# A two-layer hybrid decoder trunk: seven turned operands a layer through VectorE and DRAM, and another order of the column groups

## The chip, the cores and the metric

The kernel runs on one core of a Trainium2 chip. A core has a matrix engine (TensorE, PE in the profile; its weight loads are listed apart as PEld), three engines for element work (VectorE or DVE, ScalarE or ACT, GpSimd or POOL) and SyncE (SP), whose queue here issues nearly all transfers. Each engine works through its own instructions in order, and semaphores tie the engines together. On-chip data lie in SBUF (128 partitions); TensorE writes to PSUM.

The metric is the device time of one execution in microseconds; less is better.

## The reference

Two layers, 256 positions, width 1024, all in float32. In each layer one projection of the normalised input gives ten groups of 512 columns, three branches work on them, and a second projection adds the result to x:

```python
h = rms_norm(x, norm_g[l])
proj = h @ w_in[l]
q_a, k_a, v_a, q_h, f_h, i_h, q_m, z = jnp.split(proj, split_points, axis=-1)
# q_a, k_a: per-head RMS norm and partial rotary; 8 heads of 64
o_a = moba_attention(qa, ka, va).reshape(B, S, G)
o_h = hgrn2_chunkwise(q_h, f_h, i_h, lb_all[l])         # 4 heads of 128, gated recurrence
o_h = rms_norm(o_h, hgrn_o_norm[l])
kv_m = rms_norm(mem, mem_norm_g[l]) @ w_mem_kv[l]
o_m = memory_attention(rms_norm(q_m), rms_norm(k_m), v_m)  # 4 heads of 128, 256 memory tokens
y = jnp.concatenate([o_a, o_h, o_m], axis=-1) * jax.nn.silu(z)
x = x + y @ w_out[l]
```

With 256 positions and blocks of 256, MoBA has one block, so its attention is a plain causal one within it.

## The kernel before

**Weights.** All weight matrices stream through SBUF in 120 chunks of 128x1024 floats (512 KB). SyncE loads a chunk into `wr` (four buffers), ScalarE rounds it into `wh` (line 161, or 164 with a gain), VectorE makes the remainder `wl = wr - wh` (line 173, or 176 with a gain); `wh` and `wl` have three buffers each. A product is three matmuls: high x high, high x low, low x high. `slot` (line 206) runs twice a chunk: once a chunk it issues the next load, cast and remainder (`dma_to`, `h_to`, `l_to`: 5, 3 and 2 chunks ahead), and then `step` advances each of the active generators by one. So a `yield` in the code is about half a chunk of TensorE's time, and `yield 2` two halves.

**Groups.** `group_a` computes a column group with the result transposed (columns on partitions: F, Q, ZA, ZM), `group_b` with positions on partitions (KA, QA, IH, ZH, QM, VA). When a group's matmuls are out, a generator takes its accumulator: `g_f`, `g_q` and `g_hgrn` (the recurrent branch, "the scan"), `g_qk` (q and k of MoBA, then `g_moba` and its two `g_moba_unit`), `g_ih`, `g_va`, `g_zh` and `g_zt` (gates), `g_qm` (the memory's q, then two `g_mem_unit`), and at the start of a layer `g_km` and `g_vm` (the memory's k and v). Z stands for the gates, A, H and M for MoBA, HGRN and memory. The order of the groups in a layer is F Q ZA ZM KA QA IH ZH QM VA, then `w_out_phase` in the order H, A, M of the branches.

**Turned operands.** The norms need positions on partitions and the products need the head's columns there, so several tensors are transposed between. Five places do it on TensorE, 128x128 against `ident`, into a PSUM tile `sd` from which ScalarE and VectorE copy:

- `g_km`, line 611: kn, 8 transposes a layer, then `kmh` (line 612, with the gain) and `kml` (line 613);
- `g_qk`, line 919: k and q, 8 each, then `kT`, `qT` by ScalarE (line 920);
- `y_transpose`, line 731: zh (the gated output of HGRN), 8, then `yh`, `yl` (lines 734 and 735, with the gain of the out-norm);
- `g_qm`, line 1047: qm, 8, then `qmh`, `qml` (lines 1048 and 1049);
- `g_mem_unit`, line 1101: the softmax P of two heads, 8 transposes a unit, 16 a layer, then `PTh`, `PTl` (lines 1103 and 1104).

A sixth place, P of MoBA in `g_moba_unit`, goes another way: `across` (line 88). VectorE turns 32x32 blocks from the tensor into `blk` (one buffer, line 92), SyncE writes `blk` to a DRAM tile `there` (line 96) and reads it back by four transfers (line 99) that put the blocks on their partitions. The turned tensor then has its positions in an order of 32-wide pieces, and the matmul reads it through an access pattern of such pieces.

**What orders the work.** The instructions are traced in the order of the code; the build then orders each engine's queue by a simulated time line (`schedule_with_timeline_sim=True`), except those marked with `keep_in_program_order` (weight loads, matmuls of `mm_row`, the end of the last projection). Waits on names in `done` and on rooms (`room`, `take`) hold a generator back in the code: `P` has two tiles, `PTh` and `PTl` one each, `blk` one. The tag `qk` (one buffer) holds kn, kr of k, kr of q and qm in turn. The unit of MoBA waits before its exponentials until the gates ZM are done (line 964).

Of the kernel before, what the change touches and what calls it, by code (L numbers as in the profile page):

```python
# [45 lines left out]
def hymba_kernel(ctx: ExitStack, tc: tile.TileContext, x, mem, mem_t, positions, w_in, w_out, w_mem_kv,  # L46
# [34 lines left out]
    def rel(what="sd", n=1):  # L81
        held[what] -= n
# [5 lines left out]
    def across(dst, src, n):  # L88
        yield from room("blk")
        held["blk"] += 1  # L90
        blk = sb.tile([128, 4, n * 32], F32, name="blk", tag="blk", bufs=1)
        nc.vector.transpose(blk.rearrange("p c (n i) -> p c n i", n=n),
                            src.rearrange("p (n c i) -> p c n i", n=n, c=4))
        yield 2
        there = away.tile([4, 32, 4, n * 32], F32, name="there", tag="there", bufs=2)
        nc.sync.dma_start(there.rearrange("q j c r -> (q j) c r"), blk)
        yield 2
        for c in range(4):
            nc.sync.dma_start(dst[c * 32:c * 32 + 32], there[:, :, c].rearrange("q j r -> j q r"))
            if c % 2:  # L100
                yield
        rel("blk")

# [460 lines left out]
    def heads(t, n):  # L564
        return t.rearrange("p (h d) -> p h d", h=n)
# [13 lines left out]
    def g_km(l, acc):  # L579
# [23 lines left out]
        kmh = sb.tile([128, 4, 256], F32R, name="kmh", tag="kmh", bufs=1)  # L603
        kml = sb.tile([128, 4, 256], F32R, name="kml", tag="kml", bufs=1)
        g = gkq[:, l:l + 1]
        for t in range(2):
            ts = slice(t * 128, (t + 1) * 128)
            yield from room("sd")
            pt = side_tile()
            for h in range(4):  # L610
                nc.tensor.transpose(pt[:, h * 128:(h + 1) * 128], kn[:, t, h * 128:(h + 1) * 128], ident)
            nc.scalar.activation(kmh[:, :, ts], heads(pt, 4), AF.Copy, scale=g)
            nc.vector.scalar_tensor_tensor(kml[:, :, ts], in0=heads(pt, 4), scalar=g, in1=kmh[:, :, ts].bitcast(F32),
                                           op0=OP.mult, op1=OP.subtract)
            rel()
# [111 lines left out]
    def y_transpose(l, t, gain):  # L727
        yield from room("sd")
        pt = side_tile()
        for j in range(4):  # L730
            nc.tensor.transpose(pt[:, j * 128:(j + 1) * 128], zh[:, t, j * 128:(j + 1) * 128], ident)
        p3 = heads(pt, 4)
        oh, ol = (a[:, :, t * 128:(t + 1) * 128] for a in y_tiles(H_))
        nc.scalar.activation(oh, p3, AF.Copy, scale=gain)
        nc.vector.scalar_tensor_tensor(ol, in0=p3, scalar=gain, in1=oh.bitcast(F32), op0=OP.mult, op1=OP.subtract)
        rel()
        yield
        if t == 1:
            for k in range(4):
                done.add(f"y{4 * H_ + k}_{l}")  # L740


    def g_hgrn(l):
# [129 lines left out]
        yield 2  # L873
        for t in range(2):
            yield from y_transpose(l, t, gT[:, GR_O + l:GR_O + l + 1])


    def g_qk(l, q, acc):
# [35 lines left out]
        o = sb.tile([128, 4, 256], F32, name=tg, tag=(f"yl{M_}", f"yh{M_}")[q], bufs=1)  # L914
        for t in range(2):
            yield from room("sd")
            pt = side_tile()
            for p in range(4):
                nc.tensor.transpose(pt[:, p * 128:(p + 1) * 128], kr[:, t, p * 128:(p + 1) * 128], ident)  # L919
            nc.scalar.copy(o[:, :, t * 128:(t + 1) * 128], heads(pt, 4))  # L920
            rel()
            yield
# [28 lines left out]
    def g_moba_unit(l, u, P, mx):  # L951
# [12 lines left out]
        while f"z{M_}{l}" not in done:  # L964
            yield
# [36 lines left out]
    def g_moba(l):  # L1002
# [26 lines left out]
    def g_qm(l, acc):  # L1029
# [12 lines left out]
        for t in range(2):  # L1042
            ts = slice(t * 128, (t + 1) * 128)
            yield from room("sd")
            pt = side_tile()
            for h in range(4):
                nc.tensor.transpose(pt[:, h * 128:(h + 1) * 128], qm[:, t, h * 128:(h + 1) * 128], ident)
            nc.scalar.copy(qmh[:, :, ts], heads(pt, 4))
            nc.vector.tensor_tensor(qml[:, :, ts], heads(pt, 4), qmh[:, :, ts].bitcast(F32), op=OP.subtract)
            rel()  # L1050
# [6 lines left out]
    def g_mem_unit(l, u, qm, r, nr):  # L1057
# [35 lines left out]
        yield 2  # L1093
        yield from take("PTh", "PTl")
        PT = [sb.tile([128, 2, 2, 256], F32R, name=n, tag=n, bufs=1) for n in ("PTh", "PTl")]
        for b in range(2):
            yield from room("sd")
            pt = side_tile()
            for i in range(2):
                for t in range(2):  # L1100
                    nc.tensor.transpose(pt[:, i * 256 + t * 128:i * 256 + (t + 1) * 128],  # L1101
                                        P[:, t, i, b * 128:(b + 1) * 128], ident)
            nc.scalar.copy(PT[0][:, b], heads(pt, 2))
            nc.vector.tensor_tensor(PT[1][:, b], heads(pt, 2), PT[0][:, b].bitcast(F32), op=OP.subtract)
            rel()
# [86 lines left out]
    for l in range(DEPTH):  # L1192
# [4 lines left out]
        for gen in (A_, M_, lambda l, a: g_qk(l, 1, a), lambda l, a: g_qk(l, 0, a), g_ih, g_zh, g_qm, g_va):  # L1197
# [56 lines left out]
```

## Time and profile before

| | us |
|---|---|
| median of 3 runs | 403.14 |
| lowest and highest of them | 403.0, 404.85 |
| the profiled execution | 402.83 |
| its span in the trace | 401.0 |
| busy: TensorE, VectorE, ScalarE, GpSimd | 393.9, 310.4, 257.6, 56.4 |

The span is what the trace covers; 1.83 us of the execution lie around it. The granted clock is full (tenths of 9 or more in all slices of the page). A row of the groups reads: line, engine, operation, what it writes and reads, shapes, count, then busy time, mean ns of one, and idle time of the engine just before such instructions with what ended it. Busy time of TensorE counts overlapping instructions once; the mean of a matmul is its own length, which overlaps that of its neighbours, so what one costs is read from the distance of the starts or from the chain that ended last.

### The profile page before, as it was taken

To read this page: it belongs to the slowest core of one execution; us is meant where nothing else is said; L and a number is where in the kernel's file an instruction comes from. 1 tells how busy PE (TensorE), PEld (TensorE's weight loads), DVE (VectorE), ACT (ScalarE), POOL (GpSimd) and SP (SyncE) were. 2 spreads that over 40 slices of the span, in tenths; PEclk is the share of its full clock that TensorE was granted. 3 is DMA by queue.
4 is the path that set the end of the run, shared out by engine and by line. 5 is a ranking of instruction groups with operands and counts; after the bars stand their busy time and mean duration, and the time that the engine had idled before them with its cause. 6 is when DMAs were issued, how large, how long until landed. Compare 5 with 4: busy or idle time off the path is not lost.

```text
span 401.0 us, 7633 instructions
## 1 busy us (share of the span) xinstructions
PE 393.9 (98%) x2919; PEld 330.7 (82%) x2919; DVE 310.4 (77%) x602; ACT 257.6 (64%) x431; POOL 56.4 (14%) x79
## 2 busy tenths in 40 slices
PE   8999999999999999999999999999999999999996
PEld 5888888888887878888888888888888888787885
DVE  5789999978845989685676789898767658988653
ACT  6998757784556895553466676566654598748430
POOL 2014400605400011100000040000144001020000
PEclk9999999999999999999999999999999999999999
DMA  7976563544453397744454555634455427894402
GB/s 286 412 282 218 182 209 139 181 157 161 159 189 126 135 232 267 259 142 146 162 194 158 197 170 196 208 112 160 159 184 185 159 61 254 252 279 153 156 2 105
DMA packets 22629, 74.06 MB, mean 185 GB/s; under 512 B 2752, under 2 KB 5184, under 8 KB 22592
## 3 DMA queue, kind: packets, MB, share of 16 engines
q1 hardware_dynamic: 22304, 73.41, 54.3%
q8 instruction: 23, 0.38, 0.4%
q10 hardware_dynamic: 288, 0.15, 0.2%
q14 instruction: 14, 0.11, 0.1%
HBM read 69.36 MB, written 4.19 MB: 183 GB/s over the span
## 4 chain that ended last, share of the span: by engine, by line
PE 87%; DVE 8%; issue 1%; DMA 1%; POOL 1%; ACT 1%; DVEq 0%
PE acc L215 59%; PE acc L1138 16%; PE sd L215 5%; PE sd L219 3%; DVE wl L173 3%; DVE P L978 2%; DMA gT<-in_gains_dram 1%; PE sd L1101 1%; PE sd L428 1%; PE sd L919 1%; DVE zh L868 1%; POOL hgr L576 1%; DVE P L932 1%; ACT P L969 1%; DVE ssh L570 1%
## 5 line engine op out<-in xcount | busy, mean ns | idle before, releaser
L161 ACT CAST wh<-wr 128x1024 fp32r<-128x1024 f32 x104 | 109.2, 1052 | 85.2 <-PE acc L215 64.0
L173 DVE TENSOR_TENSOR wl<-wr,wh 128x1024 fp32r<-128x1024 f32 x104 | 126.9, 1221 | 39.5 <-ACT wh L161 39.0
L215 PE MATMUL acc<-wh,hT 128*128 128x512 f32 x384 | 123.0, 395 | 0.0
L215 PEld LDWEIGHTS acc<-wh,hT 128*128 128x128 f32 x384 | 71.8, 188 | 15.9 <-issue 1.3
L215 PE MATMUL acc<-wl,hT 128*128 128x512 f32 x192 | 75.8, 395 | 0.6 <-DVE wl L173 0.6
L215 PE MATMUL acc<-hT,wh 128*128 128x512 f32 x256 | 65.3, 395 | 0.0
L215 PEld LDWEIGHTS acc<-hT,wh 128*128 128x128 f32 x256 | 45.9, 189 | 8.6 <-ACT kn L583 0.4
L215 PEld LDWEIGHTS acc<-wl,hT 128*128 128x128 f32 x192 | 36.1, 188 | 8.0 <-DVE wl L173 1.1
L215 PEld LDWEIGHTS acc<-hT,wl 128*128 128x128 f32 x256 | 34.9, 190 | 2.5
L1138 PE MATMUL acc<-wl,yh 128*128 128x512 f32 (+1 forms) x96 | 36.9, 389 | 0.0
L1138 PE MATMUL acc<-wh,yl 128*128 128x512 f32 (+1 forms) x96 | 36.3, 388 | 0.0
L215 PE MATMUL acc<-hT,wl 128*128 128x256 f32 x256 | 35.7, 282 | 0.0
L1138 PE MATMUL acc<-wh,yh 128*128 128x512 f32 (+1 forms) x96 | 35.6, 391 | 0.0
L215 PE MATMUL acc<-wh,mTh 128*128 128x512 f32 x64 | 25.0, 393 | 0.7 <-DVE mTh L367 0.7
L164 ACT ACTIVATE wh<-wr,gT 128x1024 fp32r<-128x1024 f32 (+1 forms) x21 | 19.4, 945 | 9.3 <-PE acc L215 4.2
L215 PE MATMUL acc<-wh,mTl 128*128 128x512 f32 x64 | 24.8, 390 | 0.0
L176 DVE SCALAR_TENSOR_TENSOR wl<-wr,gT,wh 128x1024 fp32r<-128x1024 f32 (+1 forms) x21 | 20.9, 1027 | 4.6 <-ACT wh L164 4.4
L887 POOL TENSOR_TENSOR rka<-msa,pw 128x8 f32<-128x8 f32 x4 | 11.8, 2958 | 69.3 <-DVE msa L886 69.3
L1138 PEld LDWEIGHTS acc<-wh,yh 128*128 128x128 f32 x96 | 18.0, 188 | 3.6 <-issue 0.2
L1138 PEld LDWEIGHTS acc<-wl,yh 128*128 128x128 f32 x96 | 18.1, 188 | 3.5
L1138 PEld LDWEIGHTS acc<-wh,yl 128*128 128x128 f32 x96 | 18.1, 188 | 3.5
L215 PE MATMUL acc<-wl,mTh 128*128 128x512 f32 x64 | 20.2, 392 | 0.0
(219 smaller groups left out, 579.1 us busy)
## 6 DMA issues: line engine op xcount, KB each, us to landing
wr<-in_w_in_dram SPq DMA_DIRECT2D x80, 512.0 KB, 3.4
wr<-in_w_out_dram SPq DMA_DIRECT2D x24, 512.0 KB, 4.1
wr<-in_w_mem_kv_dram SPq DMA_DIRECT2D x15, 512.0 KB, 4.3
there<-blk SPq DMA_DIRECT2D x4, 768.0 KB, 3.8
PT<-there SPq DMA_DIRECT2D x16, 192.0 KB, 5.4
xs<-in_x_dram SPq DMA_DIRECT2D x2, 512.0 KB, 7.9
memr<-in_mem_dram SPq DMA_DIRECT2D x2, 512.0 KB, 6.7
out_dram<-xs SPq DMA_DIRECT2D x3, 256.0 KB, 2.0
```

The lines of the kernel that those rows point to most:

```text
L161: nc.scalar.copy(whs[i], raws[i])
L164: nc.scalar.activation(whs[i][:, sl], raws[i][:, sl], AF.Copy, scale=gT[:, g:g + 1])
L173: nc.vector.tensor_tensor(wls[i], raws[i], whs[i].bitcast(F32), op=OP.subtract)
L176: ins = nc.vector.scalar_tensor_tensor(wls[i][:, sl], in0=raws[i][:, sl], scalar=gT[:, g:g + 1], in1=whs[i][:, sl].bitcast(F32), op0=OP.mu ...
L215: nc.tensor.matmul(o, lhsT=a, rhs=b, start=s, stop=e)
L219: tc.keep_in_program_order(nc.tensor.matmul(o, lhsT=a, rhs=b, start=True, stop=True))
L428: ins = nc.tensor.transpose(pt[:, j * 256 + t * 128:j * 256 + (t + 1) * 128], xn[t][:, k * 128:(k + 1) * 128], ident)
L570: nc.vector.tensor_reduce(dst, heads(sq, n), AX.X, OP.add)
L576: nc.gpsimd.tensor_tensor(r, ms, pw[:, :n], op=OP.pow)
L887: nc.gpsimd.tensor_tensor(r[:, t8], ms[:, t8], pw[:, :8], op=OP.pow)
L978: nc.vector.tensor_scalar(P[:, i, kc[t]], P[:, i, kc[t]], ri[:, c:c + 1], None, op0=OP.mult)
L1138: ins = nc.tensor.matmul(a, lhsT=y, rhs=wt[:, cs], start=n == (0 if to is None else nk - 2) and j == 0, stop=n == nk - 1 and j == 2)
```

## The change

Six tensors more take the way of `across`: kn, k, q, zh, qm, and P of the memory's units (seven calls a layer beside MoBA's two). `turned` turns a tensor in place, from and back into the same buffer. `strips` and `strip_of` are the access patterns for the order of pieces that results. For q, zh and qm `unstripped` copies the pieces back into the old layout (ScalarE the high part, VectorE the remainder); k, km and the memory's PT stay in pieces, and the matmuls that read them do so through `strips` or `cols`. The pauses within `across` are shorter, with none between its four reads. The gain of the HGRN out-norm moves from zh's copy into the weight chunks of the second projection. MoBA's units no longer wait for ZM. The column groups come in the order F Q KA IH QA ZH QM VA ZA ZM.

```diff
@@ across @@
-        yield 2
+        yield
         there = away.tile([4, 32, 4, n * 32], F32, name="there", tag="there", bufs=2)
         nc.sync.dma_start(there.rearrange("q j c r -> (q j) c r"), blk)
         yield 2
         for c in range(4):
             nc.sync.dma_start(dst[c * 32:c * 32 + 32], there[:, :, c].rearrange("q j r -> j q r"))
-            if c % 2:
-                yield
         rel("blk")
+    def turned(a):
+        yield from across(a.rearrange("p (q r) -> p q r", q=4), a, 8)
+        yield 3
+    def strips(a):
+        return a.rearrange("p (q t h i) -> p h t q i", q=4, t=2, h=4)
+    def strip_of(o, t):
+        return o[:, :, t * 128:(t + 1) * 128].rearrange("p h (q i) -> p h q i", q=4)
+    def unstripped(oh, ol, a):
+        for t in range(2):
+            src, to = strips(a)[:, :, t], strip_of(oh, t)
+            nc.scalar.copy(to, src)
+            if ol is not None:
+                nc.vector.tensor_tensor(strip_of(ol, t), src, to.bitcast(F32), op=OP.subtract)
@@ chunks @@
-        for c in (ZA, ZM, KA, QA, IH, ZH, QM, VA):
+        for c in (KA, IH, QA, ZH, QM, VA, ZA, ZM):
...
-            chunks.append(("O", dram(w_out, (l * DMIX + kt * 128) * D, [[D, 128], [1, D]]), None))
+            chunks.append(("O", dram(w_out, (l * DMIX + kt * 128) * D, [[D, 128], [1, D]]),
+                           GR_O + l if kt // 4 == H_ else None))
@@ g_km @@
-                nc.tensor.transpose(pt[:, h * 128:(h + 1) * 128], kn[:, t, h * 128:(h + 1) * 128], ident)
-            nc.scalar.activation(kmh[:, :, ts], heads(pt, 4), AF.Copy, scale=g)
...
+        flat = kn.rearrange("p t s -> p (t s)")
+        yield from turned(flat)
+        nc.scalar.activation(kmh, flat, AF.Copy, scale=g)
+        nc.vector.scalar_tensor_tensor(kml, in0=flat, scalar=g, in1=kmh.bitcast(F32), op0=OP.mult, op1=OP.subtract)
@@ y_transpose, now y_turned @@
+        flat = zh.rearrange("p t s -> p (t s)")
+        yield from turned(flat)
+        unstripped(*y_tiles(H_), flat)
@@ g_qk @@
-                nc.tensor.transpose(pt[:, p * 128:(p + 1) * 128], kr[:, t, p * 128:(p + 1) * 128], ident)
-            nc.scalar.copy(o[:, :, t * 128:(t + 1) * 128], heads(pt, 4))
...
+        if q == 0:
+            yield from turned(flat)
+            o = o.rearrange("p (h s) -> p h s", h=4)
+            unstripped(o, None, flat)
+            yield 2
+        else:
+            yield from across(o.rearrange("p (q r) -> p q r", q=4), flat, 8)
+            yield 3
@@ second (and the scores of g_moba in the same way) @@
-                mm_row(ps[e][:, pi * 256:(pi + 1) * 256], qT[64 * e:64 * e + 64, 2 * u + pi, 128:256],
-                       kT[64 * e:64 * e + 64, 2 * u + pi])
+                mm_row(ps[e][:, pi * 256:(pi + 1) * 256].rearrange("p (t q i) -> p t q i", t=2, q=4),
+                       qT[64 * e:64 * e + 64, 2 * u + pi, 128:256], strips(kT)[64 * e:64 * e + 64, 2 * u + pi])
@@ g_moba_unit @@
-        while f"z{M_}{l}" not in done:
-            yield
@@ g_qm @@
-                nc.tensor.transpose(pt[:, h * 128:(h + 1) * 128], qm[:, t, h * 128:(h + 1) * 128], ident)
...
+        flat = qm.rearrange("p t s -> p (t s)")
+        yield from turned(flat)
+        unstripped(qmh, qml, flat)
@@ g_mem_unit @@
-                    nc.tensor.transpose(pt[:, i * 256 + t * 128:i * 256 + (t + 1) * 128],
-                                        P[:, t, i, b * 128:(b + 1) * 128], ident)
...
+        flat = P.rearrange("p t i s -> p (t i s)")
+        yield from turned(flat)
         yield from take("PTh", "PTl")
...
+        nc.scalar.copy(PT[0], flat)
+        nc.vector.tensor_tensor(PT[1], flat, PT[0].bitcast(F32), op=OP.subtract)
+        cols = [a.rearrange("p (q t n b s) -> p n b t q s", q=4, t=2, n=2, b=2) for a in PT]
```

More of the change, by code (lines that the diff above doesn't have):

```diff
@@ L602, in g_km @@
         yield 3
-        kmh = sb.tile([128, 4, 256], F32R, name="kmh", tag="kmh", bufs=1)
-        kml = sb.tile([128, 4, 256], F32R, name="kml", tag="kml", bufs=1)
+        kmh = sb.tile([128, 1024], F32R, name="kmh", tag="kmh", bufs=1)
+        kml = sb.tile([128, 1024], F32R, name="kml", tag="kml", bufs=1)
         g = gkq[:, l:l + 1]
[L606 to L611, printed above, removed]
-            nc.scalar.activation(kmh[:, :, ts], heads(pt, 4), AF.Copy, scale=g)
-            nc.vector.scalar_tensor_tensor(kml[:, :, ts], in0=heads(pt, 4), scalar=g, in1=kmh[:, :, ts].bitcast(F32),
-                                           op0=OP.mult, op1=OP.subtract)
-            rel()
+        flat = kn.rearrange("p t s -> p (t s)")
+        yield from turned(flat)
+        nc.scalar.activation(kmh, flat, AF.Copy, scale=g)
+        nc.vector.scalar_tensor_tensor(kml, in0=flat, scalar=g, in1=kmh.bitcast(F32), op0=OP.mult, op1=OP.subtract)
         T["km"] = kmh, kml
@@ L725, in y_store, with y_turned @@
             done.add(f"y{4 * br + k}_{l}")
[L727 to L736, printed above, removed]
+    def y_turned(l):
+        flat = zh.rearrange("p t s -> p (t s)")
+        yield from turned(flat)
+        unstripped(*y_tiles(H_), flat)
         yield
-        if t == 1:
-            for k in range(4):
-                done.add(f"y{4 * H_ + k}_{l}")
+        for k in range(4):
+            done.add(f"y{4 * H_ + k}_{l}")
     def g_hgrn(l):
@@ L872, in g_hgrn @@
             yield
-        yield 2
-        for t in range(2):
-            yield from y_transpose(l, t, gT[:, GR_O + l:GR_O + l + 1])
+        yield from y_turned(l)
     def g_qk(l, q, acc):
@@ L913, in g_qk @@
         tg = ("qT", "kT")[q]
[L914 to L919, printed above, removed]
-            nc.scalar.copy(o[:, :, t * 128:(t + 1) * 128], heads(pt, 4))
-            rel()
-            yield
+        flat = kr.rearrange("p t s -> p (t s)")
+        o = sb.tile([128, 1024], F32, name=tg, tag=(f"yl{M_}", f"yh{M_}")[q], bufs=1)
+        if q == 0:
[6 more added lines that the diff above has]
+            yield 3
         T[tg] = o
@@ L1041, in g_qm @@
         qml = sb.tile([128, 4, 256], F32R, name="qml", tag="hF", bufs=1)
[L1042 to L1050, printed above, removed]
+        flat = qm.rearrange("p t s -> p (t s)")
+        yield from turned(flat)
+        unstripped(qmh, qml, flat)
         yield 2
@@ L1092, in g_mem_unit @@
                 nc.vector.tensor_scalar(P[:, t, i], P[:, t, i], ri[:, c:c + 1], None, op0=OP.mult)
-        yield 2
+        flat = P.rearrange("p t i s -> p (t i s)")
+        yield from turned(flat)
         yield from take("PTh", "PTl")
[L1095 to L1101, printed above, removed]
-                                        P[:, t, i, b * 128:(b + 1) * 128], ident)
-            nc.scalar.copy(PT[0][:, b], heads(pt, 2))
-            nc.vector.tensor_tensor(PT[1][:, b], heads(pt, 2), PT[0][:, b].bitcast(F32), op=OP.subtract)
-            rel()
+        PT = [sb.tile([128, 1024], F32R, name=n, tag=n, bufs=1) for n in ("PTh", "PTl")]
+        nc.scalar.copy(PT[0], flat)
+        nc.vector.tensor_tensor(PT[1], flat, PT[0].bitcast(F32), op=OP.subtract)
+        cols = [a.rearrange("p (q t n b s) -> p n b t q s", q=4, t=2, n=2, b=2) for a in PT]
         rel("P")
@@ L1196, in hymba_kernel @@
         group_a(hT, lambda h, a: g_q(l, h, a))
[L1197 removed]
+        for gen in (lambda l, a: g_qk(l, 1, a), g_ih, lambda l, a: g_qk(l, 0, a), g_zh, g_qm, g_va, A_, M_):
             if gen in (A_, M_):
```

14 lines of the change are left out of this document (7 added, 7 removed).

## The prediction

> **What bounds the kernel now.** I read the page first (busy shares, then the chain that ended last), then TensorE's list of waits.
>
> ```profile
> PE 393.9 (98%) x2919; PEld 330.7 (82%) x2919; DVE 310.4 (77%) x602; ACT 257.6 (64%) x431; POOL 56.4 (14%) x79
> PE 87%; DVE 8%; issue 1%; DMA 1%; POOL 1%; ACT 1%; DVEq 0%
> ...
> PE sd L1047 <- ACT qm L1033: 1.2, 2, 0.6
> ...
> PE acc L215 <- DVE wl L173: 0.6, 2, 0.3
> ```
>
> TensorE is busy for 393.9 of 401.0 us, the chain runs through it for 87%, and inside the kernel it waits 1.8 us: 0.6 + 0.3 us in each layer, around 148 and 344 us. So the bound is TensorE's own list of instructions, and what is taken off that list comes off the time as long as nobody else is late. The next engine is VectorE. Its share differs by stage, so I asked for the busy time of three stretches (columns: length, then busy us and instructions of PE, PEld, DVE, ACT, POOL, clock, DMA share, GB/s):
>
> ```profile
> 29.00:160.00 131.00, 130.10 (x1114) 109.84 (x1114) 109.98 (x241) 92.16 (x155) 29.84 (x41) 1.00 0.54 181
> 160.00:201.00 41.00, 41.00 (x226) 34.65 (x225) 28.39 (x49) 20.56 (x39) 1.48 (x2) 1.00 0.54 180
> 224.00:356.00 132.00, 131.10 (x1119) 110.43 (x1118) 107.73 (x211) 89.75 (x151) 18.56 (x11) 1.00 0.55 178
> ```
>
> The first and third are the ten column groups of layers 0 and 1, the second is the output projection. In the groups VectorE is 84% and 82% busy, in the projection 69%.
>
> **What the change removes: 112 transposes on TensorE.** 8 for kn, 16 for q and k, 8 for zh, 8 for qm, 16 for the memory's P: 56 a layer. Their groups, and pieces of the chain in order of time (start, us, what):
>
> ```profile
> L919 PE MATMUL sd<-ident,kr 128*128 128x128 f32 x32 | 4.5, 272 | 0.0
> L1101 PE MATMUL sd<-ident,P 128*128 128x128 f32 x32 | 4.3, 276 | 0.0
> ...
> 44.76 0.87 PE sd L611 x8
> 100.96 0.44 PE sd L919 x4
> 114.61 0.87 PE sd L919 x8
> 152.60 0.44 PE sd L731 x4
> 172.86 1.02 PE sd L1101 x8
> 181.95 0.87 PE sd L1101 x8
> ```
>
> The 272 ns is the length of one that overlaps its neighbours. In the chain eight take 0.87 us, four 0.44, so one costs 0.11 us. A layer: kn 0.87; q and k 0.44 + 0.44 + 0.87 = 1.75; zh 2 x 0.44 = 0.88; qm, of the same form, 0.87; P 1.02 + 0.87 = 1.89. Sum 6.26, two layers **12.5 us**.
>
> [...] The chain's 0.11 us decides, and the clock column reads 1.00 throughout.
>
> The 1.8 us of waits stand where qm's transposes (L1047) follow a late copy of ScalarE, and where that copy has pushed back a weight split; with no transpose there, both go, and what is late next is what the coming parts are about. TensorE's floor is 402.83 - 12.5 - 1.8 = **388.5 us** (402.83 is the profiled execution; the three plain runs have a median of 403.14).
>
> **The new matmul operands.** Scores and outputs now read kT, km and PT in runs of 32 columns with jumps between. The nearest rows:
>
> ```profile
> 169.99 2.87 PE L215 MATMUL sd<-PT,va 128*64 128x256 f32 x32
> 172.79 1.09 PE L1101 MATMUL sd<-ident,P 128*128 128x128 f32 x8
> ...
> 158.37 0.28 PE L215 MATMUL sd<-kml,qmh 128*128 128x256 f32 x1
> 158.48 0.28 PE L215 MATMUL sd<-kmh,qml 128*128 128x256 f32 x1
> ...
> 119.96 2.03 PE L219 MATMUL sd<-kT,qT 64*128 64x128 f32 x24
> 121.92 0.50 PE L215 MATMUL acc<-wh,hT 128*128 128x512 f32 x1
> ```
>
> MoBA's PT is read that way already: 16 x (256 + 128) columns in 2.80 us is 0.46 ns a column; the contiguous km takes 0.12 us for 256, 0.47 ns. I take nothing. Upper end: all doubled, 96 of the memory's x 0.12 + 2 x (1.96 + 1.06) for kT, 17.6 us; below nothing is excluded, since the columns are the same.
>
> **What VectorE gets.** Turning 128x1024:
>
> ```profile
> L92 DVE STREAM_TRANSPOSE blk<-P 128x1536 f32<-128x1536 f32 x4 | 7.1, 1772 | 0.0
> L613 DVE SCALAR_TENSOR_TENSOR kml<-sd,gkq,kmh 128x512 fp32r<-128x512 f32 x4 | 3.0, 748 | 0.1
> L1104 DVE TENSOR_TENSOR PTl<-sd,PTh 128x512 fp32r<-128x512 f32 x8 | 5.3, 686 | 0.7 <-ACT PTh L1103 0.7
> L176 DVE SCALAR_TENSOR_TENSOR wl<-wr,gT,wh 128x1024 fp32r<-128x1024 f32 x11 | 13.8, 1280 | 3.2 <-ACT wh L164 3.1
> L173 DVE TENSOR_TENSOR wl<-wr,wh 128x1024 fp32r<-128x1024 f32 x104 | 126.9, 1221 | 39.5 <-ACT wh L161 39.0
> L161 ACT CAST wh<-wr 128x1024 fp32r<-128x1024 f32 x104 | 109.2, 1052 | 85.2 <-PE acc L215 64.0 <-PE acc L1138 15.6 <-issue 5.1
> L720 DVE TENSOR_TENSOR ys<-sd,zT 128x512 f32<-128x512 f32 x8 | 5.5, 689 | 5.4 <-PE sd L215 5.4
> L1172 DVE TENSOR_TENSOR xs<-xs,acc 128x512 f32<-128x512 f32 x8 | 5.4, 686 | 4.1 <-PE acc L1138 4.1
> ```
>
> 1772 x 1024/1536 = 1.18 us, and seven a layer make 8.3 us. One full-width subtract in place of two halves saves 2 x 0.75 - 1.28 = 0.2 for km and 2 x (2 x 0.69 - 1.22) = 0.3 for P; zh's lose their factor, 0.1. Net +7.7 us a layer. The new order also pulls work into the groups: of 28.4 us in the projection, 15 chunks x 1.22 = 18.3 are weight splits and 4 x 0.69 = 2.7 the residual sums; of the other 7.4, the memory's y_store (two units, each a product and a subtract of 0.69, 2.8) must stay and at most 4.6 move ahead. So layer 0 wants 109.98 + 7.7 + 4.6 = 122.3 us in 131 - 6.3 - 0.9 = 123.8 of TensorE: 99%, or 95% if the 4.6 stay. Layer 1: 107.73 + 7.7 + 4.6 = 120.0 in 124.8, 96%. That is the tight place. The new order spreads it: KA and QA come early, so MoBA's chain from q has five groups (four chunks of 2.7 us each, so 54 us) before the projection in place of four, and ZH has four in place of two; but the k work (five kinds of instruction, among them 2 x 0.69 three times) now meets the scan of the HGRN branch, which before had ZA and ZM beside it. I call that even. POOL gets nothing, and only the order of its small powers changes.
>
> VectorE also idles for what is not ready:
>
> ```profile
> 130.37 0.20 DVE L974 RECIPROCAL ria<-sma 128x8 f32<-128x8 f32 x1 [4.45 <-ACT P L969]
> ...
> 144.56 0.35 DVE L868 SCALAR_TENSOR_TENSOR zh<-sd,hgr,zh 128x128 f32<-128x128 f32 x1 [1.79 <-POOL hgr L576]
> ```
>
> Some of this stays. The cover is the weight splits that run ahead: with three buffers a wl may be made two chunks early. A chunk of 12 matmuls takes 12 x 0.227 = 2.7 us (below), so 5.5 us, less cast and subtract of its own (1.05 + 1.22), leaves 3.2 us before TensorE stands. Where bursts and waits overrun that, I put 2 us a layer: **+4 us** in all, taken between nothing and the rival below.
>
> **ScalarE and SyncE.** ScalarE loses four copies a layer (kT's two, and P's four become two). Without the wait for ZM (lines 964 and 965) exponentials and sigmoids alternate, and each change loads a table:
>
> ```profile
> L699 ACT ACT_TABLE_LOAD x2 | 2.6, 1283 | 0.0
> 163.01 7.05 PE acc L1138 x31
> ```
>
> At most six more a layer, 15 us over the run, against 143 us that ScalarE is idle; only the late casts would be felt, so nothing is added. SyncE gets 14 x 5 transfers:
>
> ```profile
> wr<-in_w_in_dram SPq DMA_DIRECT2D x80, 512.0 KB, 3.4
> ...
> there<-blk SPq DMA_DIRECT2D x4, 768.0 KB, 3.8
> PT<-there SPq DMA_DIRECT2D x16, 192.0 KB, 5.4
> ...
> SPq L99 <- DMA there<-blk: 5.1, 4, 2.3
> ...
> 137.36 0.33 SPq L96 DMA_DIRECT2D there<-blk  x1
> 138.47 2.06 SPq L136 DMA_DIRECT2D wr<-in_w_in_dram  x2
> 140.94 1.28 SPq L99 DMA_DIRECT2D PT<-there  x3
> ```
>
> Issues cost 0.33 + 4 x 0.43 = 2.0 us and the wait for the store 5.1/4 = 1.3, so weight loads queue some 3.3 us behind a turn. With four raw buffers, the chunk that fills a freed one is cast three chunks, 8.2 us, later, and a load lands in 3.4, so 4 us cover it. Bytes: the groups of a layer move 131 us x 181 GB/s = 23.7 MB now, and seven turns of 2 x 0.52 MB make it 31 MB in 124 us, 250 GB/s; the share of the transfer engines goes from 0.54 to about 0.75, which I take as room enough.
>
> A round trip takes 0.3 + 3.8 + 1.7 + 5.4 = 11.2 us from store to last landing (smaller transfers: somewhat less). The code leaves five slots (half chunks, 1.36 us) from store to use, 6.8 us. What reads too early is the copy on ScalarE and the subtract on VectorE, with the next casts and subtracts of weights behind them, up to 4.4 us. The build orders each queue by a simulated time line, and the rows above show weight loads put into the store's wait, so I expect most of it filled.
>
> [...]
>
> **Sum:** 388.5 + 4 = **392.5 us**.
>
> **Rivals.**
> 1. *Nothing is late*: 388.5. For it: in before, TensorE lost only 1.8 us; against it: 96 to 99% VectorE.
> 2. *Round trips show.* Twelve of the fourteen turns feed ScalarE and VectorE. If the queues aren't filled, each stands 4.4 us against 3.2 of cover, 1.2 us each: 12 x 1.2 = 14 on 388.5, 403 (no change). Partly filled, 396.
> 3. *VectorE becomes the bound* (the slower side). In the groups it idles 21 us of 131 now, in layer 1 24 of 132, waiting for casts, powers and exponentials. If it still idles 12 us a layer, layer 0 takes 122.3 + 12 - 123.8 = 10.5 us too long, layer 1 120.0 + 12 - 124.8 = 7.2: 388.5 + 17.7 = 406. The time passes that of before where 2 x idle - 1.5 - 4.8 = 14.3, at 10.3 us a layer. Against it: the 4.6 us may stay in the projection, where 41 - 28.4 = 12.6 us are free, and much of the idle time is a VectorE that has run ahead of the casts (39.5 us before the splits of L173), which a busier one no longer does.
> 4. *Reading in runs costs*: full price 406; the PT rows speak against it.
> 5. *It doesn't do what it says*: q, zh, qm, kn are still written in the same layout and no transpose of theirs remains, so the 112 do go; the part that may fail is hiding them.
>
> **Chances.** Forecast (390 to 397) 0.56; rival 1 (388 to 390) 0.10; rival 2 0.15 (half at 396 to 400.8, half about 403); rival 3 0.15; rival 4 0.04. A difference under 0.5% (2 us of 402.8) can't be told from no change. Faster: 0.56 + 0.10 + 0.08 = 0.74, some of rivals 3 and 4 falling short, 0.76; same 0.10; slower 0.14. The range goes from 387.5 (1 us under the floor, for what the chain's pieces leave uncounted) to 404, which takes in rivals 1 and 2 and leaves out rival 3 and the full price of rival 4.
>
> **What would show it.** Right: about 2807 matmuls, TensorE busy about 381 us; lines 611, 731, 919, 1047, 1101 gone; VectorE 95% or so in the groups; small waits of TensorE for wl. Wrong: TensorE waiting for tens of us on wl or wh, with a landing or VectorE named behind; scores longer than 0.12 us per 256 columns; SyncE's weight loads late by more than 4 us.

## The result, and the profile after

The changed kernel takes 407.75 us (median of 4 runs, 407.31 to 408.23) against 403.07 for the kernel before (4 runs): a ratio of 1.0112, 95% interval 1.0093 to 1.0130. It is slower by over 1%; 392.5 was forecast. The profiled execution took 408.23 us, with a span of 406.4. The medians below count every execution, while the ratios leave out three (one each of e6, e9 and e15) that ran in a slower state of the chip.

The page of the changed kernel, busy shares and the chain that ended last:

```profile
PE 390.5 (96%) x2807; PEld 323.1 (80%) x2807; DVE 323.0 (79%) x610; ACT 258.7 (64%) x424; POOL 52.5 (13%) x79
PE 58%; DVE 16%; DMA 11%; ACT 7%; issue 4%; POOL 2%; SPq 1%; ACTq 0%; DVEq 0%
```

The 112 transposes are gone (2919 to 2807). But the chain, 87% TensorE before, is now 58% TensorE, with 16% VectorE and 11% transfers: TensorE no longer sets the pace alone. Busy TensorE fell by only 3.4 us; stretches at half clock, shown below, are part of that: the eight matmuls behind the wait in ZA take 3.40 us, where the eight before it, at full clock, took 2.00.

Stretches of the changed kernel (length, busy us and instructions of PE, PEld, DVE, ACT, POOL, clock, DMA share, GB/s), cut where its groups begin and end: groups of layer 0, its projection, groups of layer 1:

```profile
31.50:167.60 136.10, 130.79 (x1097) 108.59 (x1097) 116.33 (x252) 90.21 (x156) 26.18 (x39) 0.99 0.66 213
167.60:206.00 38.40, 37.76 (x186) 30.86 (x185) 27.90 (x42) 23.54 (x34) 0.00 (x0) 1.00 0.71 246
230.00:363.70 133.70, 130.06 (x1097) 108.91 (x1098) 113.31 (x219) 87.23 (x152) 20.40 (x12) 0.99 0.66 213
```

VectorE is 85% busy in the groups of both layers, not 96 to 99%. It is not the bound. Who is late shows in the waits of the changed kernel (in total, times, longest us):

```profile
ACT yh L115 <- DMA zh<-there: 9.9, 2, 5.2
ACT qT L115 <- DMA kr<-there: 9.6, 2, 5.8
...
PE acc L231 <- ACT wh L177: 6.1, 2, 3.2
...
ACT PTh L1091 <- DMA P<-there: 4.7, 3, 1.8
...
ACT kmh L624 <- DMA kn<-there: 3.0, 2, 1.6
...
PE sd L231 <- DMA PT<-there: 1.4, 1, 1.4
```

The waits of SyncE's queue in the same kernel:

```profile
SPq L99 <- DMA there<-blk: 51.4, 18, 4.5
```

ScalarE stands 9.9 + 9.6 + 4.7 + 3.0 = 27.2 us at landings of the new trips, and behind it TensorE stands 6.1 us at casts of weights. SyncE's wait for the store rose from 5.1 to 51.4 us. Pieces of the timeline of the changed kernel around group ZA of layer 0, ScalarE's and at the end one of TensorE's (start, length, engine, what; idle time before it in brackets), show how the landing reaches TensorE:

```profile
127.71 1.06 ACT L177 CAST wh<-wr 128x1024 fp32r<-128x1024 f32 x1 [1.70 <-PE acc L231]
134.01 1.15 ACT L115 CAST yh<-zh 128x512 fp32r<-128x512 f32 x2 [5.25 <-DMA zh<-there]
135.18 1.28 ACT L968 ACT_TABLE_LOAD   x1
136.47 0.49 ACT L968 ACTIVATE P<-P,nba,rq 128x128 f32<-128x128 f32 x1
...
138.98 0.58 ACT L968 ACTIVATE P<-P,nba,rq 128x256 f32<-128x256 f32 x1
...
139.56 1.03 ACT L177 CAST wh<-wr 128x1024 fp32r<-128x1024 f32 x1
...
140.64 3.40 PE L231 MATMUL acc<-hT,wh 128*128 128x512 f32 x8 [3.23 <-ACT wh L177]
```

ScalarE stands 5.25 us for zh's trip; then come zh's copy, a table load and MoBA's exponentials, and the next cast of weights starts at 139.56, 11.85 us after the last one started. TensorE has nothing to do for 3.23 us, until 140.64. Layer 1 has the same picture with 2.87 us. And the eight matmuls after the wait take 3.40 us, 0.43 each. The stretches of that place say why:

```profile
136.00:140.00 4.00, 1.42 (x11) 1.13 (x9) 1.50 (x9) 3.99 (x14) 0.00 (x0) 1.00 0.70 267
140.00:143.50 3.50, 2.86 (x7) 2.28 (x8) 2.84 (x9) 3.50 (x8) 0.00 (x0) 0.51 0.48 121
143.50:146.00 2.50, 2.50 (x17) 2.19 (x16) 2.50 (x4) 2.50 (x10) 0.00 (x0) 1.00 0.41 156
```

Behind the wait the granted clock is 0.51 for 3.5 us. This stand of 3.23 us so costs 1.4 us more (3.40 - 2.00: the eight such matmuls before it, from 134.47 on, took 2.00 us at full clock).

### The profile page after: what moved, and what is told of

Its sections match the earlier page's. It is cut to its first block, busy times and chain, and to the rows that moved or that the text cites. A ratio compares the mean times of both kernels' runs of the same rounds, so it can differ in the third digit from the quotient of the medians.

```text
span 406.4 us, 7544 instructions
## 1 busy us (share of the span) xinstructions
PE 390.5 (96%) x2807; PEld 323.1 (80%) x2807; DVE 323.0 (79%) x610; ACT 258.7 (64%) x424; POOL 52.5 (13%) x79
## 2 busy tenths in 40 slices
DMA packets 32709, 88.73 MB, mean 218 GB/s; under 512 B 3872, under 2 KB 13472, under 8 KB 32672
## 4 chain that ended last, share of the span: by engine, by line
PE 58%; DVE 16%; DMA 11%; ACT 7%; issue 4%; POOL 2%; SPq 1%; ACTq 0%; DVEq 0%
PE acc L231 38%; PE acc L1126 14%; DVE wl L189 5%; DMA there<-blk 4%; PE sd L231 4%; DVE blk L92 2%; DMA wr<-in_w_in_dram 2%; ACT wh L177 1%; DVE P L933 1%; DMA kr<-there 1%; POOL rka L887 1%; PE sd L235 1%; DMA PT<-there 1%; DMA gT<-in_gains_dram 1%; ACT P L968 1%
## 5 line engine op out<-in xcount | busy, mean ns | idle before, releaser
L189 DVE TENSOR_TENSOR wl<-wr,wh 128x1024 fp32r<-128x1024 f32 x96 | 116.6, 1218 | 38.3 <-ACT wh L177 38.0
L177 ACT CAST wh<-wr 128x1024 fp32r<-128x1024 f32 x96 | 100.5, 1050 | 57.8 <-PE acc L231 39.2
L231 PE MATMUL acc<-hT,wh 128*128 128x512 f32 x256 | 66.5, 403 | 6.1 <-ACT wh L177 6.1
L231 PEld LDWEIGHTS acc<-hT,wh 128*128 128x128 f32 x256 | 47.6, 194 | 15.9 <-ACT wh L177 6.5
L180 ACT ACTIVATE wh<-wr,gT 128x1024 fp32r<-128x1024 f32 (+1 forms) x29 | 28.6, 1001 | 15.9 <-PE acc L231 8.5
L231 PEld LDWEIGHTS acc<-hT,wl 128*128 128x128 f32 x256 | 35.9, 194 | 2.6
L231 PE MATMUL acc<-hT,wl 128*128 128x256 f32 x256 | 36.7, 286 | 0.0
L192 DVE SCALAR_TENSOR_TENSOR wl<-wr,gT,wh 128x1024 fp32r<-128x1024 f32 (+1 forms) x29 | 31.0, 1091 | 5.2 <-ACT wh L180 5.0
L1126 PE MATMUL acc<-wh,yh 128*128 128x512 f32 (+1 forms) x96 | 32.6, 394 | 1.2 <-ACT wh L180 1.2
L968 ACT ACTIVATE P<-P,nba,rq 128x128 f32<-128x128 f32 (+1 forms) x32 | 17.3, 542 | 0.0
```

The source lines that it names most:

```text
L177: nc.scalar.copy(whs[i], raws[i])
L180: nc.scalar.activation(whs[i][:, sl], raws[i][:, sl], AF.Copy, scale=gT[:, g:g + 1])
L189: nc.vector.tensor_tensor(wls[i], raws[i], whs[i].bitcast(F32), op=OP.subtract)
L192: ins = nc.vector.scalar_tensor_tensor(wls[i][:, sl], in0=raws[i][:, sl], scalar=gT[:, g:g + 1], in1=whs[i][:, sl].bitcast(F32), op0=OP.mu ...
L231: nc.tensor.matmul(o, lhsT=a, rhs=b, start=s, stop=e)
L968: nc.scalar.activation(P[:, i, kc[t]], P[:, i, kc[t]], AF.Exp, bias=nb[:, c:c + 1], scale=rq[:, r:r + 1], accum_out=sm[:, c:c + 1])
```

## The experiments

The first theory was that the trips' latency makes the loss, through readers that stand at the head of ScalarE's queue (theory L). The rivals were the new order of the groups, VectorE's turns, and the bytes of the trips. All ratios are against the kernel before, run beside each, with 95% intervals.

**e1_order: the new order alone, transposes on TensorE.**

```diff
 # kernel before
-        for c in (ZA, ZM, KA, QA, IH, ZH, QM, VA):
+        for c in (KA, IH, QA, ZH, QM, VA, ZA, ZM):
...
-        while f"z{M_}{l}" not in done:
-            yield
...
```

> The kernel before with the new order of groups and without MoBA's wait for ZM; all transposes stay on TensorE. If the loss is the order's (the two ZA and ZM groups, which read wh only, meet the exponentials), this alone is slower than before, about 410 us, with TensorE waiting 6 us for wh around ZA. If the loss comes from the trips through DRAM, this is 401 to 405 us, as before.

404.79 us, 1.0037 [1.0016, 1.0058]. The order alone costs some 1.4 us.

**e2_turns: the changed kernel in the old order, with the wait for ZM.**

```diff
-        for c in (KA, IH, QA, ZH, QM, VA, ZA, ZM):
+        for c in (ZA, ZM, KA, QA, IH, ZH, QM, VA):
...
```

> The changed kernel with the old order F Q ZA ZM KA QA IH ZH QM VA and the wait for ZM. If the trips cost, this is no faster than 403 us and rather slower than the changed kernel (trips closer together), 405 to 415, with ScalarE waiting for landings. If the order was at fault, it is about 390 to 395.

446.59 us, 1.1051 [1.0992, 1.1110], far over the 405 to 415 that were expected. Its waits:

```profile
PE sd L231 <- DVE PTl L1094: 23.7, 2, 12.4
...
ACT PTh L1093 <- DMA P<-there: 17.7, 3, 6.7
...
PE acc L1128 <- ACT yh L115: 10.5, 2, 5.6
```

In the old order the turned operands lie so near their readers that TensorE stands 12 us at a time. The new order isn't a gain of its own; it is what the trips need, and it doesn't give them all they need.

**e3_no_trips and e4_nowhere: VectorE's turns without the transfers, and the transfers into a tile that nobody reads.**

```diff
 # e3: across() for the new tensors turns into blk (k straight into kT) and issues no transfer
-            yield from across(o.rearrange("p (q r) -> p q r", q=4), flat, 8)
+            yield from across(None, flat, 8, False, o.rearrange("p (c r) -> p c r", c=4))
 # e4: turned() reads back into junk
-        yield from across(a.rearrange("p (q r) -> p q r", q=4), a, 8)
+        yield from across(junk.rearrange("p (q r) -> p q r", q=4), a, 8)
```

> The changed kernel with VectorE's turns but without the 14 new trips (no store, no reads; the readers take the tensors as they stand, k is written by VectorE). If the trips cost, 388 to 392 us. If VectorE or the order is the bound, 400 or more.

> The changed kernel with all trips, but those of kn, q, zh, qm and P end in a tile that nobody reads, so no reader waits for a landing (k's is as in the changed kernel). If the readers' waits on ScalarE and VectorE carry the loss, about 390 us as without trips; if SyncE's waits for the stores and the load on the transfer engines carry it, about 403 to 408 us.

e3 took 396.10 us, 0.9808 [0.9763, 0.9854]; e4 394.77, 0.9782 [0.9744, 0.9821]. The page and the waits of e4:

```profile
PE 384.5 (98%) x2807; PEld 319.1 (81%) x2807; DVE 322.9 (82%) x610; ACT 258.8 (66%) x424; POOL 52.1 (13%) x79
...
SPq L99 <- DMA there<-blk: 40.8, 17, 3.9
```

e4 has every turn, every byte, every issue and 40.8 of the 51.4 us of SyncE's waits, and it is 13 us faster than the changed kernel. What it lacks is that a reader, or the next writer of the tensor, depends on the landing (k's trip, and that of MoBA's P as before, have their real readers). So the loss comes with the dependence, not with VectorE's turns, bytes or issues; the build orders the queues of e4 anew as well, and what that alone does is among the 13 us and wasn't separated. With the dependence gone the change brings about what was forecast, 394.8 for 392.5.

Where the 13 us lie is read from the starts of the accumulating matmuls in the two profiled executions: each column is the matmul that comes at the same place in the count, in the changed kernel the first of its group (in e4 eight of ZA's run before VA's last, from 127.70 on, and from 319.25 in layer 1; worked out from the traces, us):

```
             layer 0: F      VA      ZA      ZM  projection | layer 1: F      VA      ZA      ZM  projection   last
e4_nowhere        29.42  115.62  129.97  143.86  158.87         220.94  307.17  321.52  335.40  350.73   387.56
changed           31.50  118.10  134.47  151.84  167.61         229.86  316.08  331.28  348.54  363.66   401.98
```

2.1 us are there at the start and come from the clock (last section). From F to VA the two run alike, to 0.4 us. From VA to the projection the changed kernel loses 8.74 - 2.48 = 6.3 us in layer 0 and 12.93 - 8.91 = 4.0 in layer 1, and in layer 1's projection 1.5 more. The two spans, 406.4 and 392.0 us, differ by 14.4: by the pages TensorE is idle 8.4 us longer (15.9 against 7.5) and busy 6.0 us longer, of which the start makes 2.1 and the two stretches at half clock about 3.

**e5_zh_nowhere, e6_q_nowhere, e8_zh_pe: one tensor's trip out of the way.**

```diff
 # e5 (zh) and e6 (q): only this tensor's trip ends in junk
-        yield from turned(flat)
+        yield from turned(flat, junk)
 # e8: zh by TensorE, as before
+                nc.tensor.transpose(pt[:, j * 128:(j + 1) * 128], zh[:, t, j * 128:(j + 1) * 128], ident)
```

> The changed kernel; the trip of zh alone ends in a tile that nobody reads, the others are real. If ScalarE's wait for zh's landing, with the late casts and the exponentials behind it, is the loss, about 398 to 400 us and TensorE's two waits of about 3 us at ZA are gone. If every reader costs its share (five kinds), 405 us.

> The same with q's trip in place of zh's. If zh's is the loss, 406 to 408 us as the changed kernel; if all readers cost alike, 405; if q's (ScalarE waits 9.6 us for it in two places) is the one, 400 or less.

> The changed kernel with zh transposed on TensorE as before (16 more transposes, 1.8 us); six turns a layer remain. If zh's wait is the loss, 399 to 402 us. If all turns share in it, 407 or more.

e5: 407.27 us, 1.0104 [1.0072, 1.0135]. e6: 403.45, 0.9990 [0.9970, 1.0010]. e8: 409.95, 1.0157 [1.0131, 1.0183]. TensorE's longest wait in e5 and in e8:

```profile
PE sd L233 <- DMA PT<-there: 5.2, 2, 2.9
```

```profile
PE sd L231 <- DMA PT<-there: 5.3, 3, 2.9
```

ScalarE's stand at zh, and TensorE's two stands in ZA, are gone, and nothing is gained: the wait is now at MoBA's PT, one step later. That was a miss for theory L in its simple form. Only q's trip gives back 4.3 us, and it stands ahead of MoBA's whole chain: in e6 zh is turned at 121.30 us and MoBA's first P at 140.60, in the changed kernel at 124.66 and 145.02.

**e7_late, e14_early, e12_pin, e13_pin_late: when and in which order the readers come.**

```diff
 # e7: yield 7; e14: yield 1; e12: as is; e13: yield 6 (in turned)
-        yield 3
+        yield 7
 # e12, e13: unstripped() and PTh, PTl keep their place in the code's order
-            nc.scalar.copy(to, src)
+            pin(nc.scalar.copy(to, src))
```

> The changed kernel with four more pauses (half chunks) between the reads of a turn and its reader, for all turns in place. If the loss is that a reader stands at the head of ScalarE's queue before its data land, 395 to 400 us: later readers, no wait. If it is the chain of the turned tensors to the projection that is too long, slower than the changed kernel, 410 or more.

> The changed kernel with one pause in place of three between the reads and the reader. If the standing of readers costs, slower than the changed kernel, 410 us or more; if the length of the chain costs, faster, 403 to 406.

> The changed kernel with the readers of the turned q, zh, qm and P held in the order of the code on ScalarE and VectorE, so that none is put ahead of a cast or split that was traced before it. If readers that were queued too early cost, 398 to 402 us; if only the length of the trips in the chain costs, 407 to 412.

> The same with six pauses in place of three between the reads and the reader. If the standing of readers at the head of a queue costs, the best of all, 395 to 400 us; if the length of the chain costs, slower than the one before it.

e7: 417.66, 1.0361 [1.0340, 1.0382]; e14: 411.00, 1.0203 [1.0134, 1.0272]; e12: 408.60, 1.0116 [1.0077, 1.0156]; e13: 425.22, 1.0522 [1.0470, 1.0573]. A longer pause in the code was meant to give the landing time. ScalarE's stand at zh became longer, 19.6 us in place of 9.9; a shorter one (e14) made it 12.4. The pause moves the code's order, but the build still puts the reader in ScalarE's queue ahead of its landing. The row of e7:

```profile
ACT yh L115 <- DMA zh<-there: 19.6, 2, 10.0
```

In e12 the readers are held where the code has them. ScalarE no longer stands at zh, q or qm, and ZA runs without a stand. The waits of e12:

```profile
PE sd L233 <- DMA PT<-there: 7.0, 2, 3.9
...
ACT PTh L1093 <- DMA P<-there: 6.6, 4, 2.2
```

The loss has moved to MoBA's PT in ZM, and the total is that of the changed kernel. With longer pauses on top (e13) TensorE stands 4.2 and 4.1 us at PT, and each chain ends later still, in the projection:

```profile
PE acc L1128 <- ACT yh L733: 6.7, 4, 2.4
...
ACT wh L179 <- DMA wr<-in_w_out_dram: 21.3, 10, 4.4
```

So a landing that isn't waited for must still be early enough for the chain behind it.

**e9_pool, e15_poolq, e11_blk2: other resources.**

```diff
 # e9: the readers of q, zh, qm and P on GpSimd
-            nc.scalar.copy(to, src)
+            nc.gpsimd.tensor_copy(to, src)
...
 # e15: the new trips' transfers issued by GpSimd
+        q = nc.gpsimd if n == 8 else nc.sync
 # e11: a turn buffer and DRAM tiles of their own for the 1024-wide turns
-        blk = sb.tile([128, 4, n * 32], F32, name="blk", tag="blk", bufs=1)
+        blk = sb.tile([128, 4, n * 32], F32, name="blk", tag=f"blk{n}", bufs=1)
```

> The changed kernel; the copies and subtracts that read the turned q, zh, qm and P go to GpSimd, which is idle 87% of the time, in place of ScalarE and VectorE. All trips are real. If what costs is that casts and splits of weights stand behind readers that wait for a landing, 395 to 399 us. If the length of the chain through the trips costs, 405 us or more, since GpSimd's copies are slower.

> The changed kernel with the transfers of the seven new turns issued by GpSimd in place of SyncE, so that no weight load stands behind a wait for a store. By the trips to nowhere SyncE's waits cost nothing, so 405 to 410 us; if with readers they do matter (late weights, late casts), 398 to 403.

> The changed kernel with a turn buffer and a DRAM tile of their own for the seven new turns, so that MoBA's two and the new ones don't queue for one buffer. If trips in a row make the chain too long, 400 to 403 us. If the readers' waits cost, about 407 us as the changed kernel.

e9: 413.99, 1.0224 [1.0153, 1.0296]; e15: 425.81, 1.0522 [1.0450, 1.0595]; e11: 411.86, 1.0195 [1.0152, 1.0238]. In e9 no weight cast stands behind a landing of q, zh, qm or P, and TensorE's largest wait is in the projection, at the memory's output. ScalarE's wait for the weights of w_out, the second row, tells little: e4, faster than the kernel before, has nearly as much of it (third row).

```profile
PE acc L1126 <- ACT yh L731: 5.0, 4, 1.7
...
ACT wh L177 <- DMA wr<-in_w_out_dram: 13.2, 6, 4.0
```

```profile
ACT wh L179 <- DMA wr<-in_w_out_dram: 11.5, 6, 4.2
```

GpSimd is slower at this, too: its subtract for the memory's PT took 2.87 us, VectorE's 1.23 in the changed kernel. So e9 lengthens the memory's chain by itself, and doesn't say what the stands alone cost.

In e15 SyncE is free of the new trips, but from GpSimd's queue the stores and most of the reads land later. Transfers of e15 (count, KB, median us from issue to landing), and of the changed kernel:

```profile
there<-blk POOLq DMA_DIRECT2D x14, 512.0 KB, 5.0
...
P<-there POOLq DMA_DIRECT2D x16, 128.0 KB, 4.9
```

```profile
there<-blk SPq DMA_DIRECT2D x14, 512.0 KB, 3.6
...
P<-there SPq DMA_DIRECT2D x16, 128.0 KB, 3.0
```

Issuing from another engine brought no gain here: the store took 5.0 us for 3.6, the reads of P 4.9 for 3.0. TensorE's largest waits in e15 are 8.3 us at the memory's `yh`, 4.6 at PT and 3.8 at zh; how much of its 18 us over the changed kernel comes from the later landings wasn't separated.

e11 brings no gain (it is 4.1 us slower than the changed kernel, and why slower stays open). That a second buffer doesn't help there has its reason in VectorE's timeline of the changed kernel (layer 0; the row of MoBA's first P is the last):

```profile
124.66 1.23 DVE L92 STREAM_TRANSPOSE blk<-zh 128x1024 f32<-128x1024 f32 x1
130.66 1.24 DVE L92 STREAM_TRANSPOSE blk<-qm 128x1024 f32<-128x1024 f32 x1
...
145.02 1.77 DVE L92 STREAM_TRANSPOSE blk<-P 128x1536 f32<-128x1536 f32 x1
```

P's turn comes 14 us after qm's. It waits not for the buffer but for P itself, whose exponentials began at 136.47, behind ScalarE's stand at zh, and whose scaling by `ria` ended at 143.97. With the second buffer it starts at 144.71.

**e10_kn_k, e17_old_kn_k: only kn and k through DRAM, in the new order and in one near the old.**

```diff
 # kernel before, with g_km and k's half of g_qk as in the changed kernel; e10 in the order of e1
-        for c in (ZA, ZM, KA, QA, IH, ZH, QM, VA):
+        for c in (ZA, KA, ZM, QA, IH, ZH, QM, VA):   # e17, with the wait for ZM
```

> The kernel before in the new order, with only kn and k turned through DRAM (32 transposes fewer, 3.5 us; k has no reader on ScalarE, kn's is far from its use); q, zh, qm and P stay on TensorE. If a turn pays where no cast stands behind its reader, 401 to 402 us, 3 under the order alone. If any trip costs as much as its transposes, 404 to 406.

> The kernel before with the old order but KA one group earlier (F Q ZA KA ZM QA IH ZH QM VA) and the wait for ZM, and only kn and k turned through DRAM. Theory: a turn pays where nothing that reads it is near; both are read far behind. 32 transposes fewer are 3.5 us: 399 to 401 us, faster than before and than the new order with the same two turns. If k's trip is too close to q's scores here, 403 or more.

e10: 401.86, 0.9963 [0.9937, 0.9989]; e17: 401.56, 0.9958 [0.9935, 0.9980]. These two trips have distant readers and pay, by 1.5 and 1.7 us against the kernel before. e17's order is not faster than e10's, as had been expected. From e1 to e10, 32 transposes at 0.11 are 3.5 us, and 2.9 were gained.

**e16_kn_k_zh, e18_two_blk: zh in addition, first with the one turn buffer, then with two.**

```diff
 # e16: e10 with y_turned(l), its two readers held in program order, the gain in w_out's chunks
-            yield from y_transpose(l, t, gT[:, GR_O + l:GR_O + l + 1])
+        yield from y_turned(l)
 # e18: e16 with
-        blk = sb.tile([128, 4, n * 32], F32, name="blk", tag="blk", bufs=1)
+        blk = sb.tile([128, 4, n * 32], F32, name="blk", tag=f"blk{n}", bufs=1)
```

> The kernel before in the new order with kn, k and zh turned through DRAM, zh's readers held in the order of the code; q, qm and P on TensorE. zh is read by the second projection only, four groups later, so its turn is off the chain from q: 400 us, 1.8 us under kn and k alone. If a reader that stands for a landing costs by itself, 403 or more.

> e16 (kn, k and zh through DRAM, zh's readers in program order) with a turn buffer and a DRAM tile of their own for the 1024-wide turns, so that MoBA's P and zh no longer share one. In e16 MoBA's first P is normalised by 121.3 us, but its turn starts at 135.57, behind zh's turn (130.02) and zh's store, since zh's generator had claimed the one buffer; TensorE then waits 5.4 and 4.8 us at MoBA's PT. Theory A (the shared turn buffer is what makes zh's trip dear): P is turned at about 122 to 124 us as in e10, the two waits go, and with each 3.4 us at half clock: e16's 409.6 less 10 to 12, about 398 to 401, at or below e10's 401.86. Theory B (the trip's own latency and SyncE's queue, with the weight loads behind its waits, make it dear): P is turned early, but the loss moves to zh's readers or to late weights, as it did in every edit before; 406 to 411.

e16: 409.60, 1.0150 [1.0123, 1.0177], 7.7 us worse than e10. e18: **399.69 us, 0.9920 [0.9901, 0.9939]**, as theory A had it, and the fastest of the kernels that leave nothing out. It is 2.2 us under e10 by the medians and 1.7 by the ratios, whose intervals touch, so what zh's turn adds to those of kn and k isn't clear of the spread. TensorE's waits in e16, then in e18:

```profile
PE sd L223 <- issue: 5.4, 1, 5.4
PE sd L223 <- DMA PT<-there: 4.8, 1, 4.8
```

```profile
PE sd L223 <- DMA PT<-there: 1.6, 1, 1.6
```

The reason stands in VectorE's timeline, of e16 first (P is normalised by L979, the last piece at 120.38), then of e18:

```profile
120.38 0.87 DVE L979 TENSOR_SCALAR P<-P,ria 128x256 f32<-128x256 f32 x3
...
130.02 1.24 DVE L92 STREAM_TRANSPOSE blk<-zh 128x1024 f32<-128x1024 f32 x1
...
135.57 1.78 DVE L92 STREAM_TRANSPOSE blk<-P 128x1536 f32<-128x1536 f32 x1 [1.56 <-DMA there<-blk]
```

```profile
121.97 1.77 DVE L92 STREAM_TRANSPOSE blk<-P 128x1536 f32<-128x1536 f32 x1
...
132.49 1.24 DVE L92 STREAM_TRANSPOSE blk<-zh 128x1024 f32<-128x1024 f32 x1
```

In e16, MoBA's P is ready at 121.3 and is turned at 135.57: the one buffer was kept for zh, which was ready only at 128.8. With a buffer of its own for zh, P goes at 121.97, of the two waits of 5 us one of 1.6 is left, and no other stand of TensorE over 1 us appears behind the start. So here the price of a trip was the room it held, not its latency: the second buffer is worth 9.9 us.

## Why the prediction was wrong, point by point

**The transposes, the operands in runs, the bytes: right.** 2807 matmuls are left. From start to next start the 112 transposes took 12.0 us in the trace of the kernel before (12.5 forecast), and in e4, where but for k nothing depends on the new landings, the ratio of 0.9782 is a gain of 8.8 us. 394.77 is 2.3 over the forecast and 6.3 over the floor of 388.5, of which e1 puts 1.4 on the order; TensorE is busy for 384.5 us there (381 was forecast). Matmuls that read runs of 32 columns showed no price: in e18, where kT is read so, its two kinds of score matmuls take 4.05 and 1.99 us in sum from start to next start, the same as before. In e4, where other matmuls come between them, it is 1.6 us more. Rival 4 falls. By the pages 88.73 MB were moved for 74.06, 14.7 more, as seven turns a layer of 2 x 0.52 MB make.

**The waits of 1.8 us: gone, but replaced.** TensorE now stands 6.1 us at weight casts where it lost those 1.8.

**VectorE: +4 us forecast, and rival 3 at 406: the size was not far off, the rival was wrong.** Of e4's 6.3 us over the floor, 1.4 are the order, and up to 4.9 are left for VectorE and all else. The groups of layer 0 and its projection in e4, which no new landing but k's stretches, and then in the kernel before, all cut where the groups begin and end:

```profile
29.40:158.90 129.50, 128.85 (x1098) 107.69 (x1098) 115.66 (x251) 91.01 (x157) 28.10 (x43) 1.00 0.71 222
158.90:197.00 38.10, 37.37 (x185) 30.73 (x184) 28.50 (x43) 22.45 (x33) 0.00 (x0) 1.00 0.76 254
```

```profile
29.30:157.90 128.60, 127.70 (x1097) 107.61 (x1096) 107.58 (x238) 89.85 (x151) 28.22 (x39) 1.00 0.55 183
157.90:201.00 43.10, 43.10 (x241) 36.66 (x240) 30.49 (x52) 22.57 (x41) 2.79 (x2) 1.00 0.53 176
```

VectorE is 89% busy in the groups of e4, where 99% or 95% were forecast, and TensorE nearly all the time. The groups gained 8.1 us of VectorE's work and the projection lost 2.0. So VectorE has 6.1 us more in this layer, where 7.7 were forecast, and of the 4.6 that might move into the groups about 2.0 did. The forecast's 99% has a slip besides: it takes all 6.3 us of transposes off the groups, but the memory's P, 1.9 of them, stood at 172.86 and 181.95, in the projection; without it the two shares would have been 97% and 94%. That the time landed near rival 3's 406 is chance; its mechanism didn't occur.

**ScalarE's tables: right.** At most twelve further loads were allowed for; there are 14 where there were 11, and one of them, 1.28 us, is part of the 11.85 us in ZA.

**SyncE: right in e4,** which carries 40.8 us of its waits and takes no longer than e3, which has none of the new trips. The DMA share was forecast at 0.75 in the groups and is 0.66 in both layers of the changed kernel, 0.71 in layer 0 of e4; in the projection of layer 0, for which nothing was forecast, it is 0.71.

**The round trip: the step that failed.** The prediction put the reader up to 4.4 us before its landing and went on: "so I expect most of it filled", with a cover of 3.2 us behind it; so the sum has no term for the trips, which cost 13 us. The lateness was about right: ScalarE stands 5.0 us at each landing of zh and 4.8 at q's. Three other things were not.
- It wasn't filled. The build put the readers in ScalarE's queue ahead of the landings, and there they stand at its head, 27.2 us in all with those of kn and P. More pause in the code (e7) doesn't change that.
- The price isn't the lateness less the cover. In ZA the cast of weights stands behind the landing, and behind what had been piled up by it: a table load and the exponentials. From 5.25 us of standing came 3.23 us of a stopped TensorE, where 5.25 - 3.2 = 2.0 would have been the rule of rival 2, and then 3.4 us at half clock.
- Above all, a trip was priced at its own reader. Each one also makes the chains late that come after it: q's makes MoBA's late (e6 gives 4.3 us back), zh's stand delays MoBA's exponentials (136.47 us; 134.11 in e5 and 131.30 in e8) and so its own trips (its first P is turned at 145.02, 142.85 and 142.68), and the memory's P ends in the projection. When the stand is removed, the loss comes up at PT (e5, e8, e12) or at `yh` in the projection (e9). Rival 2 had the right mechanism at a price of at most 14 us over the floor; it was 13 us over e4, on top of the 6 that e4 itself stands over the floor, so 19.

**The chances.** Slower had 0.14, nearly all of it VectorE's. The end that came true, round trips beyond 403, had no chance of its own, because the rival stopped at one stand a trip.

What stays open: how the 13 us divide between the trips of q, zh, qm and P in the changed kernel. With its landing sent nowhere, q's trip alone gives 4.3 us back and zh's alone 0.5; qm's and P's were not tried alone, and each edit lets the build order the queues anew. For zh it is settled in a smaller kernel: e16 and e18 differ in the turn buffer and its DRAM tile alone. e18 with q's, qm's or the memory's trips added was not tried.

## What to carry to other kernels

Price a round trip through memory by the chain that waits behind it and by the buffer and queue that it holds, not by its own reader's wait: send everything "to nowhere" first to see what the dependence alone costs, then put trips back one by one, with the most distant readers first. When removing a wait doesn't move the total, the chain behind it is late, and the next place to look is when its first operand was ready and what it then stood for. Of the 112 transposes, the 48 of kn, k and zh together were worth taking off TensorE with a turn buffer for each size of turn (e18, 0.992 of the time before); for q, qm and P that wasn't shown.

## What the runs showed of the hardware

**Half clock at stands of TensorE.** At each of TensorE's two stands of about 3 us in the changed kernel (3.23 and 2.87) the granted clock went to one half for 3.413 us, at 140 and 338 us; in e2 it did so for 3.4, 3.4, 17.07, 6.8 and 17.07 us, once, once, five times, twice and five times 3.413. The mean clock falls with it: 0.991 in the changed kernel, 0.945 in e2, 1.000 before. In ZA of layer 0 the half clock made a stand of 3.23 us dearer by 1.4 us (3.40 us for eight matmuls, 2.00 before). The length of the stand alone didn't decide in these traces: stands of 3.04 us in e9 (to 363.69) and 2.94 in e7 (to 167.57) kept the full clock, and one of 1.92 us in e15 (to 328.94) was followed by half clock.

**The start of the full clock varies between executions.** Stretches 8 to 10 us of the changed kernel, then of the kernel before:

```profile
8.00:10.00 2.00, 2.00 (x6) 1.53 (x5) 1.66 (x3) 1.89 (x4) 0.00 (x0) 1.00 1.03 386
```

```profile
8.00:10.00 2.00, 2.00 (x10) 1.69 (x9) 2.00 (x4) 1.83 (x4) 0.00 (x0) 1.00 1.05 408
```

Six matmuls where there were ten: in the changed kernel they start 0.43 us apart from 7.45 to 9.16 us and 0.23 from 10.63 on, in the kernel before 0.23 from 6.86 on. In the clock's own records full speed began at 10.35 us in this execution and at 4.6 to 5.7 in the profiled ones of before and of e1 to e4, though the stretch's clock column shows 1.00. That is the 2.1 us that the changed kernel has lost before F. Two other traces support it: in e6 and e10 half clock came back from 7.85 to 11.26 and from 7.42 to 10.84 us, and F starts at 31.78 and 31.76, in the changed kernel at 31.50; in the other 17 traces it starts at 29.26 to 30.36. Whether the other runs of the changed kernel share it, no record tells. Over the traces, full speed was first granted between 4.0 us (e10) and 10.35.
